# Residual of a Strassen down projection: added in SBUF pages, or by accumulating transfers in DRAM

## The chip, the cores and the metric

The kernel runs on one core of one Trainium2 chip. The metric is the device time of one launch in microseconds (us). A profile of one execution gives the time of every instruction. Engines are named as the profile names them: PE (matrix products; PEld loads its weights), DVE (vector), ACT (scalar), POOL (GpSimd), SP (which only issues transfers here).

## The reference

A decoder block on x of 1024 tokens by 1024 features, all in float32; the part that matters is the SwiGLU layer, which stands at the start and at the end of the block (a mixer of convolution and attention lies between):

```
def swiglu(x, w_gu, w_down):
    g, u = jnp.split(x @ w_gu, 2, axis=-1)
    return (jax.nn.silu(g) * u) @ w_down

u = modulate(rmsnorm(h, norm1_g[l]), mod[:, 0, 0], mod[:, 0, 1])
h = h + FFN_RES_WEIGHT * mod[:, 0, 2][:, None, :] * swiglu(u, ffn1_w_gu[l], ffn1_w_down[l])
...
h = h + FFN_RES_WEIGHT * mod[:, 2, 2][:, None, :] * swiglu(u, ffn2_w_gu[l], ffn2_w_down[l])
return rmsnorm(h, final_g)
```

The hidden width is 2816, 22 tiles of 128. h is the residual.

## The kernel before

Activations lie transposed, features on the 128 partitions and tokens along the free axis. A float32 number is split into a high and a low part for the PE (ACT casts the high part, DVE subtracts it for the low part: `put_split`, L110 to L112), and a product is three matmuls of 512 columns per tile of 128: high by high, high by low, low by high. A high part alone is enough for the first of the three.

SBUF is kept in pages of 128 x 1024 floats, in rings by tag: R has 8 pages, U 16, H 8, X 4. A tile that asks for a page gets the next one of its ring, once its last user is done with it.

Hidden tiles 2 to 21 are worked in ten pairs by Strassen's scheme in Winograd's form: `strassen` makes seven products instead of eight. The seven operands of the moving side are named B11, T2, B21, T3, T1, T4 and B22, in the order of the products. Each product goes to a PSUM bank of one of four tags ("za" has three banks, "fb" two, "dn" two, "st" one), and `u1` (a copy by ACT, L319) to `u4` gather the sums by which the four blocks of the result come out. `sink` takes a block.

`Ffn.pair` makes the hidden tiles of a pair p; `keep(p)` forms their sums in pages called ha, hb, ta and tb (in ring R) and stores the seven operands to DRAM in `hd`. `Ffn.down` is the down projection of these pairs, in three groups: pairs 0 to 3, 4 to 6 and 7 to 9. For a group it loads the seven operands of each pair (L445), splits them, and then runs `strassen` for q = 0 to 3, two tiles of output features each. Names begin with f in the first FFN and s in the second: fB11_0 is operand B11 of pair 0, fd00a to fd00g are the seven split weight blocks for group 0 and q = 0, fd00T1 is the bank of that product, and fd01, fd02, ... follow. POOL makes the sums of weights for each of them (L280, L297, four operations, the first named s3).

The residual lies in the eight R pages while `down` runs: each is loaded in the first group (L457), and `sink` makes a block in three steps: DVE adds two sums (L464), ACT scales by the gate (L465), DVE adds the block to the R page (L466). After the groups the remaining two hidden tiles are done by halves of the tokens (the products named dn): DVE adds each to R (L504), ACT squares, and POOL sums the squares for the norm behind.

The order of the instructions on each engine is set when the program is built, by a scheduler with a timeline of its own that may put a product ahead of another of the same `strassen`; each engine then runs its list in order, and so does SP with the transfers it issues.

## Time and profile before

| what | us |
|---|---|
| median of 3 runs (lowest, highest) | 2101.79 (2100.91, 2103.1) |
| span of the profiled execution | 2098.4 |
| what lies around the span, by the median | 3.4 |
| busy PE, DVE, ACT, POOL in the span | 2039.0, 1600.0, 907.4, 698.1 |
| down projection, groups of the first FFN: from about | 466 to 671 |
| down projection, groups of the second FFN: from about | 1851 to 2053 |

The page gives the profiled execution's span, from its first to its last instruction; its time as a launch is not given apart, so the median stands for it. Busy PE is a modelled figure: matmuls are pipelined. The two stretches of the last lines are where the change works.

### The profile page before, as it was taken

The numbers are of one execution on the slowest core, as the hardware profiler recorded it, in microseconds if no ns is written. First come the engines' busy times: TensorE is split into PE (matmuls) and PEld (weight loads), VectorE is DVE, ScalarE is ACT, GpSimd is POOL, SyncE is SP. The second block draws the span as 40 slices with busy tenths as digits, with TensorE's granted clock in tenths as the row PEclk, the third lists the DMA queues.
The fourth block names the chain that finished last, engine by engine and source line by source line (L and its number), as shares of the span: only waits on it lengthen the run. The fifth ranks groups of instructions, "written<-read, shape, count | busy, mean of one in ns | idle before, by whom it ended". The sixth has DMA issues, their size and how long they took to land.

```text
span 2098.4 us, 26171 instructions
## 1 busy us (share of the span) xinstructions
PE 2039.0 (97%) x8964; PEld 1644.0 (78%) x8964; DVE 1600.0 (76%) x2299; ACT 907.4 (43%) x1601; POOL 698.1 (33%) x510
## 2 busy tenths in 40 slices
PE   7999999999999999999999999999999999999996
PEld 4788888887788788887777788888888888878785
DVE  7858878878998896668876664639766767698998
ACT  4532332353654653226555552337332332355554
POOL 3125455453232333532221100032344444332433
PEclk8999999999999999999999999999999999999998
DMA  8117646565543334244443268321222223375332
GB/s 310 72 56 259 237 181 221 223 218 187 178 143 105 129 146 155 81 119 119 112 138 100 89 233 304 130 108 46 86 95 102 104 101 116 105 278 191 109 97 83
DMA packets 129943, 307.98 MB, mean 147 GB/s; under 512 B 12689, under 2 KB 23057, under 8 KB 129810
## 3 DMA queue, kind: packets, MB, share of 16 engines
q1 hardware_dynamic: 129810, 306.31, 42.2%
q8 instruction: 71, 1.16, 0.2%
q14 instruction: 62, 0.51, 0.1%
HBM read 224.47 MB, written 81.79 MB: 146 GB/s over the span
## 4 chain that ended last, share of the span: by engine, by line
PE 80%; DVE 10%; ACT 3%; issue 3%; DMA 2%; POOL 1%; SPq 0%; DVEq 0%; ACTq 0%; POOLq 0%
PE bga L142 4%; PE bgb L142 4%; PE bo L142 3%; PE z L142 3%; PE byb L142 2%; PE t L851 2%; PE bya L142 2%; PE fbu L142 1%; PE fbg L142 1%; PE o L861 1%; PE o L862 1%; PE sdn L142 1%; DVE wa L204 1%; DVE fT L112 1%; DVE fo L597 1%
## 5 line engine op out<-in xcount | busy, mean ns | idle before, releaser
L830 POOL TENSOR_SCALAR_AFFINE_SELECT a<-a 128x128 f32<-128x128 f32 x64 | 48.2, 761 | 224.7 <-ACT a L730 220.8
L204 DVE SCALAR_TENSOR_TENSOR wa<-wa,cb 128x1024 f32<-128x1024 f32 x72 | 95.6, 1334 | 6.7 <-DMA wa<-in_w_ada_dram 6.7
L833 DVE TENSOR_TENSOR_SCAN r<-r 128x128 f32<-128x128 f32 (+3 forms) x64 | 87.9, 1378 | 1.2
L233 POOL TENSOR_TENSOR acc<-acc,sqc 128x512 f32<-128x512 f32 x14 | 21.0, 1501 | 187.1 <-ACT sqc L232 187.1
L730 ACT ACTIVATE r<-z 128x512 f32<-128x512 f32 (+2 forms) x96 | 47.0, 495 | 53.0 <-PE z L142 52.5
L280 POOL TENSOR_TENSOR fw<-fw 128x512 f32<-128x512 f32 x18 | 29.3, 1626 | 98.0 <-DVE fp10d L112 48.4
L855 ACT CAST ah<-t 128x512 fp32r<-128x512 f32 (+1 forms) x96 | 45.7, 485 | 32.2 <-PE t L851 21.1
L856 DVE TENSOR_TENSOR al<-t,ah 128x512 fp32r<-128x512 f32 (+1 forms) x96 | 51.2, 547 | 9.9 <-ACT ah L855 9.2
L836 DVE TENSOR_TENSOR a<-a,r 128x127 f32<-128x127 f32 (+3 forms) x64 | 48.4, 758 | 10.6 <-POOL a L830 8.6
L465 ACT ACTIVATE fd<-fd,mod 128x512 f32<-128x512 f32 x48 | 34.6, 724 | 35.0 <-DVE fd L464 34.7
L465 ACT ACTIVATE sd<-sd,mod 128x512 f32<-128x512 f32 x48 | 34.6, 723 | 34.9 <-DVE sd L464 34.4
L730 ACT ACTIVATE a<-z 128x512 f32<-128x512 f32 (+2 forms) x96 | 46.7, 497 | 6.5 <-PE t L851 6.3
L280 POOL TENSOR_TENSOR sw<-sw,sw 128x512 f32<-128x512 f32 x20 | 29.1, 1456 | 60.3 <-issue 38.2
L829 DVE TENSOR_TENSOR r<-r,mask 128x128 f32<-128x128 f32 x64 | 18.8, 298 | 39.4 <-ACT r L730 39.2
L851 PE MATMUL t<-ident,a 128*128 128x128 f32 x288 | 48.2, 276 | 0.1
L424 POOL TENSOR_TENSOR sha<-sha,sg 128x512 f32<-128x512 f32 x20 | 34.7, 1734 | 33.4 <-DVE sha L423 33.4
L424 POOL TENSOR_TENSOR shb<-shb,sg 128x512 f32<-128x512 f32 x20 | 30.6, 1532 | 42.3 <-DVE shb L423 42.3
L142 PE MATMUL z<-KB,Q 64*128 64x512 f32 (+2 forms) x96 | 41.2, 435 | 0.5 <-DMA KB<-qk_d 0.5
L947 DVE SCALAR_TENSOR_TENSOR res<-bo,mod,res 128x512 f32<-128x512 f32 x16 | 12.0, 748 | 38.0 <-PE bo L142 38.0
L417 ACT ACTIVATE fg<-fg 128x512 f32<-128x512 f32 x36 | 22.8, 632 | 41.3 <-DVE fg L416 41.1
L851 PEld LDWEIGHTS t<-ident,a 128*128 128x128 f32 x288 | 33.8, 140 | 8.6 <-issue 2.9
L466 DVE TENSOR_TENSOR sr<-sr,sd 128x512 f32<-128x512 f32 x48 | 36.2, 760 | 5.1 <-ACT sd L465 5.0
(3251 smaller groups left out, 6680.3 us busy)
## 6 DMA issues: line engine op xcount, KB each, us to landing
wa<-in_w_ada_dram SPq DMA_DIRECT2D x72, 512.0 KB, 8.3
sw<-in_w_gu_dram SPq DMA_DIRECT2D x40, 512.0 KB, 3.4
fw<-in_w_gu_dram SPq DMA_DIRECT2D x36, 512.0 KB, 4.2
fT<-fhd_d SPq DMA_DIRECT2D x40, 256.0 KB, 5.3
sT<-shd_d SPq DMA_DIRECT2D x40, 256.0 KB, 5.4
qk_d<-qk SPq DMA_DIRECT2D x16, 512.0 KB, 4.5
fB<-fhd_d SPq DMA_DIRECT2D x30, 256.0 KB, 5.9
sB<-shd_d SPq DMA_DIRECT2D x30, 256.0 KB, 5.6
```

The lines of the kernel that those rows point to most:

```text
L142: mm = nc.tensor.matmul(out, l, r, start=first and i == 0, stop=last and i == n - 1)
L204: nc.vector.scalar_tensor_tensor(out=w, in0=w, scalar=1.0, in1=cb, op0=ALU.mult, op1=ALU.mult, accum_out=mods[m][:, nb:nb + 1])
L280: eng.tensor_tensor(out=out, in0=a, in1=b, op=ALU.subtract)
L424: nc.gpsimd.tensor_tensor(out=h[i], in0=h[i], in1=g[i], op=ALU.mult)
L465: act(out=t, in_=t, func=AF.Identity, scale=g)
L730: act_last["silu"] = act(func=AF.Sigmoid, **kw).ins
L830: nc.gpsimd.affine_select(out=a[:, d], in_=a[:, d], pattern=[[-1, P]], compare_op=ALU.is_gt, fill=0.0, base=0, channel_multiplier=1)
L833: nc.vector.tensor_tensor_scan(out=c, data0=c, data1=c, initial=1.0, op0=ALU.mult, op1=ALU.bypass)
L836: nc.vector.tensor_tensor(out=c, in0=c, in1=r[:, tot + 1:tot + W], op=ALU.mult)
L851: act_last['att'] = nc.tensor.transpose(tb[:, (i - 4 * hf) * P:(i - 4 * hf + 1) * P], a[:, off + j * P:off + (j + 1) * P], ident).ins
L855: nc.scalar.copy(out=ah[:, :w], in_=tb[:, c])
L856: nc.vector.tensor_sub(out=al[:, :w], in0=tb[:, c], in1=ah[:, :w].bitcast(F32))
```

## The change

The residual is no longer held in pages during the groups. It stands in DRAM in `res_d` (for the first FFN a copy of x, made by eight transfers from DRAM to DRAM at the start of the pairs; for the second FFN the buffer that the mixer wrote). `sink` loses its third step: POOL issues a transfer that adds the block to its place in DRAM, 48 of them for each FFN, 256 KB each. After the last group the eight R pages are loaded from DRAM, and the tail goes on as before. Operand B11 takes its pages from ring R instead of U.

```
@@ -431,9 +431,10 @@
-        def down(self, src, done, keep=None, final=False):
+        def down(self, res, done, keep=False, final=False):
             n = self.nm
-            tags = dict(self.tags, T1="H", T3="H")
+            tags = dict(self.tags, T1="H", T3="H", B11="R")
@@ -451,11 +452,6 @@
-                    if gi == 0:
-                        for dt in (2 * q, 2 * q + 1):
-                            R[dt] = page("R", f"{n}r{dt}")
-                            dma(out=R[dt], in_=src[dt])
@@ -463,11 +459,14 @@
                         act(out=t, in_=t, func=AF.Identity, scale=g)
-                        nc.vector.tensor_tensor(out=R[dt][:, c], in0=R[dt][:, c], in1=t, op=ALU.add)
+                        nc.gpsimd.dma_start(out=res[dt, :, c], in_=t, accum_op=ALU.add)
                     strassen(*w, k, B, ("za", "st")[q % 2], f"{n}d{gi}{q}", sink)
                 off += 2 * k * P
+            for dt in range(KT):
+                R[dt] = page("R", f"{n}r{dt}")
+                dma(out=R[dt], in_=res[dt])
@@ -503,8 +502,8 @@
-                    if keep is not None:
-                        dma(out=keep[dt, :, c], in_=R[dt][:, c])
+                    if keep:
+                        dma(out=res[dt, :, c], in_=R[dt][:, c])
@@ -618,26 +617,29 @@
+        res_d = dram.tile([KT, P, T], F32, name="res_d")
         for p in range(1, len(PAIRS)):
             f1.pair(p)
             if p < 8:
                 ada(p + 1, "R")
+            else:
+                for kt in range(4 * (p - 8), 4 * (p - 7)):
+                    dma(out=res_d[kt], in_=xT[kt])
-        res_d = dram.tile([KT, P, T], F32, name="res_d")
-        f1.down(xT, norm2, res_d)
+        f1.down(res_d, norm2, keep=True)
```

The last call, `f2.down(res2_d, final, final=True)`, stays as it is.

Outside the down projections no engine's list changes but for the copies at the start and a few products that trade places. Inside, the lists change as follows. On PE, at the first group of the first FFN, before (one row of each product; x3 is high by high, high by low and low by high for one pair):

```order
L142 MATMUL fd00B11_3855<-fB11_0_3705,fd00a_3825 128x512 x3
...
L142 MATMUL fd00T2_3869<-fT2_0_3721,fd00b_3833 128x512 x3
...
L142 MATMUL fd00B21_3883<-fB21_0_3737,fd00d_3836 128x512 x3
...
L142 MATMUL fd00T3_3900<-fT3_0_3753,fd00c_3828 128x512 x3
...
L142 MATMUL fd00T1_3914<-fT1_0_3769,fd00e_3842 128x512 x3
...
L142 MATMUL fd00T4_3932<-fT4_0_3785,fd00f_3845 128x512 x3
...
L142 MATMUL fd00B22_3949<-fB22_0_3801,fd00g_3848 128x512 x3
...
L142 MATMUL fd01B11_4004<-fB11_0_3705,fd01a_3974 128x512 x3
```

and now:

```order
L142 MATMUL fd00T2_3873<-fT2_0_3729,fd00b_3837 128x512 x3
...
L142 MATMUL fd00B21_3887<-fB21_0_3745,fd00d_3840 128x512 x3
...
L142 MATMUL fd00T1_3918<-fT1_0_3777,fd00e_3846 128x512
L142 MATMUL fd00T4_3936<-fT4_0_3793,fd00f_3849 128x512
L142 MATMUL fd00T1_3918<-fT1_0_3777,fd00e_3846 128x512 x2
...
L142 MATMUL fd00T4_3936<-fT4_0_3793,fd00f_3849 128x512 x2
...
L142 MATMUL fd00B11_3859<-fB11_0_3713,fd00a_3829 128x512
L142 MATMUL fd00T3_3904<-fT3_0_3761,fd00c_3832 128x512 x3
...
L142 MATMUL fd00B22_3953<-fB22_0_3809,fd00g_3852 128x512 x3
...
L142 MATMUL fd00B11_3859<-fB11_0_3713,fd00a_3829 128x512 x2
...
L142 MATMUL fd00B11_3859<-fB11_3_3725,fd00a_3829 128x512 x3
L142 MATMUL fd01B11_4004<-fB11_0_3713,fd01a_3974 128x512 x3
```

B11, which was the first of the seven products, is now the last to be finished; T1 and T4 come third and fourth, and d01 begins behind B11.

On SP, from the weights of q = 1 on, before (fr0 to fr4 are residual pages; fta9 and ftb9 the stores of the last pair's sums):

```order
L452 DMA fwd0_3_3968<-in_w_ds1_dram 128x1024
L406 DMA fhd_d_157<-fhb9_3415 128x2x512
L452 DMA fwd0_4_4115<-in_w_ds1_dram 128x1024
L457 DMA fr0_3821<-in_xT_dram 128x1024
...
L457 DMA fr4_4119<-in_xT_dram 128x1024
L406 DMA fhd_d_157<-fta9_3694 128x2x512
L406 DMA fhd_d_157<-ftb9_3695 128x2x512
```

and now:

```order
L453 DMA fwd0_3_3972<-in_w_ds1_dram 128x1024
L406 DMA fhd_d_157<-fhb9_3420 128x2x512
L453 DMA fwd0_4_4115<-in_w_ds1_dram 128x1024
L446 DMA fB11_0_3713<-fhd_d_157 128x512
...
L446 DMA fB11_4_4405<-fhd_d_157 128x512
L406 DMA fhd_d_157<-fta9_3699 128x2x512
L406 DMA fhd_d_157<-ftb9_3700 128x2x512
L446 DMA fB11_5_4409<-fhd_d_157 128x512
L446 DMA fB11_6_4413<-fhd_d_157 128x512
```

The loads of B11 stand where the residual's pages were loaded, and not, as before, as the first of the group; fB11_5 and fB11_6 (group 1) stand behind the stores of ta9 and tb9, since fB11_6 takes the page of ta9.

On ACT, at the same place, now:

```order
L111 CAST fT4_3_3805<-fT4_3_3805 128x512
L111 CAST fT2_4_4417<-fT2_4_4417 128x512
...
L111 CAST fB21_4_4429<-fB21_4_4429 128x512
L111 CAST fB11_0_3713<-fB11_0_3713 128x512
L111 CAST fd01b_3982<-fwd0_2_3970 128x512
...
L111 CAST fB11_3_3725<-fB11_3_3725 128x512
L111 CAST fB11_4_4405<-fB11_4_4405 128x512
...
L111 CAST fd01f_3994<-fwd0_3_3972 128x512
L111 CAST fB11_5_4409<-fB11_5_4409 128x512
L111 CAST fB11_6_4413<-fB11_6_4413 128x512
L319 COPY fd00ot_3855<-fd00B11_3859 128x512
```

Before, the copy fd00ot (u1 of the first product) stood ahead of all this, since its product came first. Now it stands behind the casts of B11 for group 0 and of fB11_4 to fB11_6. On DVE, the low parts follow the same order: behind the last split of T4 stand, up to that of fB11_3, 15 instructions (four splits of group 1, the four sums of `keep(9)`, three weight blocks of d01, four splits of B11); before, 7 stood between there and the last split of the group, fB22_3.

On POOL, where the second group begins, now (fd0311 to fd0312 are the blocks of the last q of group 0):

```order
L462 DMA res_d_901<-fd0311_4335 128x512
L462 DMA res_d_901<-fd0322_4366 128x512
L462 DMA res_d_901<-fd0321_4384 128x512
L462 DMA res_d_901<-fd0312_4401 128x512
L280 TENSOR_TENSOR fd11s3_4621<-fwd1_2_4613,fwd1_3_4615 128x384
L297 TENSOR_TENSOR fwd1_3_4615<-fwd1_3_4615 128x384
L280 TENSOR_TENSOR fwd1_2_4613<-fwd1_3_4615,fwd1_2_4613 128x384
L462 DMA res_d_901<-fd1011_4555 128x512
L280 TENSOR_TENSOR fwd1_2_4613<-fwd1_2_4613 128x384
```

Before, the four transfers and that of fd1011 were not there; the sums of weights for d11 followed those for d10 directly. The second FFN has the same lists with s for f.

## Rows read from the trace of the kernel before

**Rows 1.** The page, parts 1 and 4: busy time by engine, and the chain.

```profile
PE 2039.0 (97%) x8964; PEld 1644.0 (78%) x8964; DVE 1600.0 (76%) x2299; ACT 907.4 (43%) x1601; POOL 698.1 (33%) x510
...
PE 80%; DVE 10%; ACT 3%; issue 3%; DMA 2%; POOL 1%; SPq 0%; DVEq 0%; ACTq 0%; POOLq 0%
```

**Rows 2.** Windows: length, busy PE, PEld, DVE, ACT, POOL, clock, DMA, GB/s.

```profile
475.00:495.00 20.00, 16.63 (x57) 12.06 (x57) 20.00 (x27) 5.08 (x10) 8.22 (x5) 0.83 0.60 218
...
560.00:580.00 20.00, 16.90 (x72) 12.85 (x71) 20.00 (x32) 8.09 (x16) 12.04 (x7) 1.00 0.23 61
...
620.00:640.00 20.00, 18.75 (x81) 14.59 (x81) 20.00 (x32) 7.95 (x15) 9.23 (x6) 1.00 0.29 79
...
1858.00:1878.00 20.00, 16.40 (x67) 11.97 (x66) 20.00 (x26) 5.49 (x10) 8.24 (x6) 1.00 0.61 221
...
1938.00:1958.00 20.00, 16.89 (x66) 12.63 (x65) 20.00 (x33) 9.86 (x20) 9.01 (x4) 0.92 0.26 74
```

**Rows 3.** Timeline of PE, first FFN, first group: start, duration, operation, [idle].

```profile
466.44 2.88 PE L142 MATMUL fd00B<-fB,fd00a 128*128 128x512 f32 x12
...
477.41 0.73 PE L142 MATMUL fd00T<-fT,fd00c 128*128 128x512 f32 x2 [0.38 <-DVE fT L112]
...
483.17 0.73 PE L142 MATMUL fd00T<-fT,fd00e 128*128 128x512 f32 x2 [2.38 <-DVE fT L112]
...
484.85 5.06 PE L142 MATMUL fd00T<-fT,fd00f 128*128 128x512 f32 x11 [0.57 <-DVE fT L112]
...
492.87 2.88 PE L142 MATMUL fd01B<-fB,fd01a 128*128 128x512 f32 x12
```

**Rows 4.** Timeline of DVE in the same stretch.

```profile
481.37 4.64 DVE L112 TENSOR_TENSOR fT<-fT 128x512 fp32r<-128x512 f32 x4
...
486.53 0.68 DVE L112 TENSOR_TENSOR fT<-fT 128x512 fp32r<-128x512 f32 x1
...
490.63 1.28 DVE L112 TENSOR_TENSOR fB<-fB 128x512 fp32r<-128x512 f32 x2
```

**Rows 5.** Timeline of SP, which issues the transfers, in the same stretch.

```profile
481.47 0.33 SPq L452 DMA_DIRECT2D fwd<-in_w_ds_dram  x1
```

**Rows 6.** Timelines of DVE and PE, second FFN, first group.

```profile
1869.47 0.68 DVE L112 TENSOR_TENSOR sT<-sT 128x512 fp32r<-128x512 f32 x1
...
1875.57 2.88 PE L142 MATMUL sd01B<-sB,sd01a 128*128 128x512 f32 x12
```

**Rows 7.** DMA issues of the whole span: count, KB each, median us to landing.

```profile
fB<-fhd_d SPq DMA_DIRECT2D x30, 256.0 KB, 5.9
...
swd<-in_w_ds_dram SPq DMA_DIRECT2D x16, 384.0 KB, 3.1
...
shd_d<-sta SPq DMA_DIRECT2D x10, 512.0 KB, 2.8
...
res_d<-fr SPq DMA_DIRECT2D x16, 256.0 KB, 2.0
...
sr<-res_d SPq DMA_DIRECT2D x8, 512.0 KB, 5.5
```

**Rows 8.** Timelines, second group: POOL and PE (first FFN), PE (second).

```profile
560.71 3.98 POOL L280 TENSOR_TENSOR fd11s<-fwd,fwd 128x384 f32<-128x384 f32 x1 [13.62 <-DMA fwd<-in_w_ds_dram]
...
568.11 0.73 PE L142 MATMUL fd11T<-fT,fd11b 128*128 128x512 f32 x2 [1.40 <-ACT fd11b L111]
...
571.20 0.70 PE L142 MATMUL fd11T<-fT,fd11c 128*128 128x512 f32 x2 [1.70 <-DVE fd10ah L322]
...
1954.50 2.77 PE L142 MATMUL sd11T<-sT,sd11b 128*128 128x512 f32 x7
```

**Rows 9.** Timelines of the tails: POOL (first FFN), ACT and DVE (second).

```profile
679.13 17.89 POOL L233 TENSOR_TENSOR facc<-facc,sqf 128x512 f32<-128x512 f32 x13 [0.68 <-ACT sqf L232]
...
2056.84 0.72 ACT L465 ACTIVATE sd<-sd,mod 128x512 f32<-128x512 f32 x1 [1.42 <-DVE sd L464]
...
2062.72 0.75 DVE L504 SCALAR_TENSOR_TENSOR sr<-sdn,mod,sr 128x512 f32<-128x512 f32 x1 [0.61 <-PE sdn L142]
```


## The prediction

> **What bounds the kernel now.** I read the page first. PE is busy for 2039.0 of the span's 2098.4 us, and the chain that ended last lies on PE for 80% and on DVE for 10% [rows 1]. So a microsecond taken from DVE, ACT or POOL is worth nothing where PE runs without a gap. The places to look for are those where PE waits in the down projections, and windows of 20 us find them: in each the busy time of DVE is to be compared with that of PE [rows 2]. Where a group begins, DVE is full (20.00 of 20) and PE is not: it lacks 3.4 us in the first group of the first FFN and 3.6 in that of the second, 3.1 at each second group, 1.25 at the third group of the first FFN. At the first group of the first FFN and the second group of the second FFN the granted clock falls too (0.83, 0.92). Then the timelines show who is late. In the first group PE waits for the low parts of T3, T1 and T4, one split of DVE each [rows 3], and DVE makes these back to back, 0.60 us apart [rows 4]. Inside a group PE has no such gaps.
>
> **Adds and transfers.** 48 adds of DVE per FFN go. They lie beside PE's products and give nothing by themselves, except at a group's start, counted below. 48 accumulating transfers per FFN come, on POOL. The eight copies of x are issued on SP long before, with PE on the pairs; I cost them at nothing, since no load that is due soon stands behind them on SP's list and their 4 MB have the whole of the pairs to move in; PE's work there is the cover, and a wait of SP in their place would stop the next weights by about what one such transfer takes, some 5.5 for a page [rows 7], which the range's upper end holds.
>
> **The first group.** Here the lists say more than the diff. B11's pages come from ring R, where `keep(9)` still holds pages, so its loads stand behind the weights of q = 1, whose fifth page SP issued at 481.5 us [rows 5]; T2's splits are now the first. What does d00 wait for?
>
> DVE. T4_3's split has as many instructions ahead of it as before (B22's stand there in place of B11's), so it ends at 487.2 again. Behind it stand 15 up to B11_3's: 487.2 + 15 x 0.60 = 496.2, where the last split of the group ended at 491.9 before [rows 4]. PE's last matmuls then end d00 at 496.8; before, d01 began at 492.87 [rows 3]. That alone is +3.9.
>
> PE. Without B11 it runs out of work after T2 and B21, at about 472, until T1's first low part, nine splits ahead of T4_3's end, 481.6. Then 57 matmuls remain: 12.9 us at 0.227 each (12 products take 2.72 from start to start), so 494.5; with eleven of them at the slow pace that followed the shorter waits before (5.06 us for eleven, 0.46 each) 497.1 [rows 3].
>
> ACT. d01's first bank of "za" is the one that the copy fd00ot empties (B11, T3 and B22 of d00 fill all three), and that copy stands behind the cast of fB11_6, whose load waits for the page of fta9. fta9's last sum is the seventh instruction behind T4_3's split: 491.4. Its store takes 2.8, as that of the same tile in the second FFN [rows 7]: 494.2. The load is issued 0.3 later and lands after between 3.1 us (weights) and 5.9 (these operands, where many are queued at once) [rows 7]; with few transfers beside it I take 3.5, the lower end more nearly: 498.0. Two operations of ACT at 0.7 each [rows 9] give 499.4.
>
> The last of the three decides: 499.4 - 492.9 = **+6.5**. In the second FFN T4_3's split ends at 1870.1 and sd01 began at 1875.57 [rows 6]. By the same steps fta is done by 1874.5, the store at 1877.3; ftb's sum, eleventh behind T4_3, and its store's issue stand ahead of the load on SP, so the load goes at 1877.5, lands at 1881, and sd01 begins at 1882.5: **+6.9**. Bounds: DVE alone gives +3.9 and +4.1, with one copy behind it +4.7 and +4.9; a load of 5.9 gives 2.4 more in each, a slow clock on the first eleven matmuls of d01 another 2.6 in each. Together +13.4, between 8 and 23.
>
> **The second and third groups.** While DVE and ACT wait less for loads in group 0, group 1's B11 and four more operands are split there, and the adds are gone. At d11 PE waited 1.40 for fd11b (ACT's, behind POOL's sum fd11s) and 1.70 for DVE's fd10ah [rows 8]. DVE has 40 instructions to do up to there where it had 46: six at 0.60 are 3.6, so the 1.70 goes. The 1.40 I let go by 0.6 only, since four transfers of POOL now stand ahead of fd11s. So 2.3 of 3.1 at the second group of the first FFN, 0.7 of 1.25 at the third, and 2.3 of 3.1 at the second group of the second FFN, where the slow clock goes with the wait: seven matmuls took 2.77 [rows 8], 1.2 more than at 0.227, of which I take 1.0. Sum **-6.3**. At most all of it goes, 3.1 + 1.25 + 3.1 + 1.2 (-8.7), at least the two waits of 1.70 (-3.4).
>
> **The tails.** The residual's last pages are loaded behind the last transfers. The trace has none issued by POOL. From below, a store of the same 256 KB from SP lands in 2.0; from above, it may be a store and a read one after the other, 2.0 + 5.5 = 7.5 [rows 7]. I take 4.5, nearer to the store, with an issue of up to 1.3, what a sum of POOL takes (13 in 17.89) [rows 9], within it. A load of a page alone I take at 4, between 2.0 and 5.5 [rows 7]. In the first FFN PE ends the groups at about 671 and the last block is ready some 2 us behind, at 673, so the page stands at 673 + 4.5 + 4 = 681.6; POOL's chain of sums adds tile 6 at 679.13 + 4 x 1.38 = 684.6 [rows 9] and is what ends last there: nothing. In the second FFN the last scale ended at 2057.6 [rows 9]; without DVE's adds between, it comes 1.5 earlier: 2056 + 4.5 + 4 = 2064.5, and DVE wanted tile 6 at 2062.7 [rows 9]. 1.8 late, of which its waits for PE of 0.6 each take up some: **+1**, between 0 and 6.
>
> **The sum.** +13.4 - 6.3 + 1 = +8.1. The profiled span is 2098.4 and the median of the three runs 2101.79; the 3.4 around the span are not touched, so 2101.8 + 8.1 = 2109.9, and I say 2110.
>
> The Trainium skill (DMA: Bandwidth & Descriptors, "Anatomy of one DMA — SWDGE (gpsimd) path") gives about 2.0 us plus the bytes at 436 GB/s for a transfer issued by GpSimd, an estimate of 2.6 us for 256 KB. No run here shows one. By it the tail of the second FFN would cost nothing and the sum would be 2109.
>
> **Rivals.** A: POOL becomes the bound. In the groups of three pairs a q has seven products of nine matmuls, 63 x 0.227 = 14.3 us, and POOL's work there is 9 to 12 of 20 us [rows 2], 7 to 8 of 14.3; four transfers come on top. If one holds POOL for more than about 1.7 us, POOL falls behind PE. The rows near it run from SP's 0.33 for an issue [rows 5] to 3.98 for a sum of POOL beside a full DVE, where others take 1.3 to 1.4 [rows 8, 9]. At 3 us each a q takes 7.5 + 12 = 19.5 instead of 14.3; over eight such q in each FFN that is 16 x 5.2 = 83 at most, and with some slack left in each group 2130 to 2180. Against it: two blocks of a q can be under way while POOL goes on, if the issue is short as on SP. 0.11.
>
> The Trainium skill speaks for A (SBUF — State Buffer, "SBUF: two separate sides"): GpSimd writes the descriptors of its transfers through a port that DVE can lock, and starves while DVE does. That POOL's sums stretch beside DVE the trace shows (3.98 against 1.3) [rows 8, 9]; whether a transfer's issue does, no run here shows.
>
> B, on the other side: faster. The place is DVE's row of splits ahead of T4_3. There 27 instructions took 20.00 us, 0.74 each [rows 2], where 0.60 is what an undisturbed one needs [rows 4]; the rest falls together with sums of POOL. If the new order keeps them apart, T4_3 is done up to 27 x 0.14 = 3.8 earlier in each FFN, and if fB11_6 lands by DVE's floor as well, the sum is 8.0 - 7.6 - 8.7 + 1 = -7.3, 2094.5; it decides from about 2 us on in each. Against it: POOL makes the same sums of weights in that stretch. 0.14.
>
> C: no change. DVE's floor with one copy behind it decides (+9.6) and the gains come between 6.3 and 8.7: 2101.8 + 9.6 - 8.7 = 2102.7 to 2105.1. It needs fB11_6 by 496 instead of 498.0, a landing in 1.5 us, or a page that comes free earlier. That the change doesn't do what it says at the second groups, since the waits there come back by POOL's weights, is in the forecast's upper part. 0.18.
>
> **How the numbers follow.** The forecast as worked out (2106 to 2124) has 0.57; A 0.11, B 0.14, C 0.18. A measurement of this kernel tells about 0.2% (4.2 us) from no change. Slower is the forecast and A, 0.68; same is C, 0.18; faster is B, 0.14. The range leaves out nearly all of A and half of B: 2096 to 2128. The forecast alone has 2106 to 2124.
>
> **What would show it.** PE's timeline at the first groups: a wait of several us behind B21, and d01's start at 499.4 and 1882.5; then ACT's cast of fB11_6 ahead of fd00ot. At the second groups no wait for fd10ah and some 0.8 for fd11b. POOL's rows: how long an accumulating transfer holds it, and how long it takes to land. In the second FFN's tail a wait of DVE for a load at tile 6. The prediction is wrong if d01 begins before 497, if POOL is late for PE inside a group, or if the tail waits for more than one load.

## The result, and the profile after

The changed kernel takes 2139.77 us, median of four runs (2137.66 to 2141.68), where the kernel before takes 2101.76 beside it: a ratio of 1.0172, 95% interval 1.0156 to 1.0188. The forecast was 2110 with a range of 2096 to 2128; the sign was right, the size was not. The profiled span went from 2098.4 to 2136.7, 38.3 us more. The page after, parts 1, 3, 4 and 5 (to be laid beside [rows 1]):

```profile
PE 2052.4 (96%) x8964; PEld 1649.2 (77%) x8964; DVE 1541.2 (72%) x2203; ACT 910.1 (43%) x1601; POOL 773.4 (36%) x606
...
q0 software_dynamic: 13824, 25.17, 7.7%
...
PE 75%; DVE 11%; DMA 5%; issue 4%; ACT 2%; POOL 2%; SPq 0%; DVEq 0%; POOLq 0%; ACTq 0%
...
L462 POOL DMA_DIRECT2D res_d<-fd x48 | 42.2, 892 | 59.8 <-ACT fd L461 53.6
```

DVE did 59 us less work, as the change means it to. POOL is busy for 36% only, and an accumulating transfer holds it for 0.89 us. What is new in the chain that ended last is DMA, 5% for 2%. Line q0 is the queue of POOL's transfers: their number of packets, megabytes, and the time that they took, as a share of all sixteen DMA engines over the span.

To see where the 38 us lie, I took the start of the first product of each stage from PE's timelines. Each column is the time from one of these starts to the next: group 0, 1 and 2 of each FFN, its tail (first product of dn to the product for the norm, in the second FFN to the end), and between the FFNs the mixer with the second FFN's pairs:

| kernel | start | f g0 | f g1 | f g2 | f tail | between | s g0 | s g1 | s g2 | s tail | span |
|---|---|---|---|---|---|---|---|---|---|---|---|
| before | 466.4 | 83.6 | 61.2 | 59.2 | 19.1 | 1162.1 | 81.2 | 62.9 | 57.4 | 45.4 | 2098.4 |
| change | 467.0 | 92.7 | 57.8 | 63.2 | 28.6 | 1164.9 | 91.3 | 57.8 | 61.6 | 51.9 | 2136.7 |
| difference | +0.6 | +9.1 | -3.4 | +4.0 | +9.5 | +2.9 | +10.0 | -5.1 | +4.2 | +6.5 | +38.3 |

So the second groups gained, by 8.5; the first groups lost 19, the tails 16, the third groups 8. The experiments ran on other chips, six by the numbers on record (7, 14, 11, 0, 8 and 13), where the kernel before takes 2107 to 2109. So each is compared by its ratio to the kernel before on the same chip, and an absolute time that an expectation gives is to be read against 2101.8. The time of a stage comes from one execution, and a part of it is PE's clock: the second group of the first FFN takes 61.2 us in this profile of the kernel before at a granted clock of 1.00, and 63.9 in the one of experiment 12 at 0.95, with PE idle for 3.1 in both. Differences of a stage below 3 us are not read one by one.

**First group.** PE's timeline, then ACT's and SP's (compare [rows 3] and [rows 5]):

```profile
467.04 2.88 PE L142 MATMUL fd00T<-fT,fd00b 128*128 128x512 f32 x12
...
475.15 0.47 PE L142 MATMUL fd00T<-fT,fd00f 128*128 128x512 f32 x1 [2.28 <-DVE fhb L423]
477.94 3.74 PE L142 MATMUL fd00T<-fT,fd00e 128*128 128x512 f32 x9 [2.32 <-DVE fT L112]
...
496.11 2.13 PE L142 MATMUL fd00B<-fB,fd00a 128*128 128x512 f32 x8 [0.78 <-DVE fB L112]
500.85 4.61 PE L142 MATMUL fd01B<-fB,fd01a 128*128 128x512 f32 x12 [2.61 <-ACT fd00ot L319]
```

```profile
499.08 1.24 ACT L111 CAST fB<-fB 128x512 fp32r<-128x512 f32 x2 [3.71 <-DVE fd01f L112]
500.22 0.58 ACT L319 COPY fd00ot<-fd00B 128x512 f32<-128x512 f32 x1
```

```profile
492.48 0.37 SPq L406 DMA_DIRECT2D fhd_d<-fta  x1
494.88 0.37 SPq L406 DMA_DIRECT2D fhd_d<-ftb  x1
495.31 2.99 SPq L446 DMA_DIRECT2D fB<-fhd_d  x3
```

The chain is the one foreseen: store of fta, store of ftb, load of B11 of group 1, its casts, and behind them the copy for which d01 waits 2.61 us. It starts d01 at 500.85 (forecast 499.4), and then d01's first twelve products take 4.61 us in place of 2.88. The granted clock of these 4.61 us is 0.63, so PE was in part at the lower of its two levels, behind waits of 0.78 and 2.61 us; before, it was 1.00 in the same stretch.

**Third group and tails.** The issues and their landing (compare [rows 7]), and pieces of the chain that ended last:

```profile
res_d<-fd POOLq DMA_DIRECT2D x48, 256.0 KB, 5.5
res_d<-sd POOLq DMA_DIRECT2D x48, 256.0 KB, 5.4
...
fwd<-in_w_ds_dram SPq DMA_DIRECT2D x16, 384.0 KB, 5.1
swd<-in_w_ds_dram SPq DMA_DIRECT2D x16, 384.0 KB, 5.0
```

```profile
642.67 4.16 DMA fwd<-in_w_ds_dram
...
657.20 6.22 DMA fwd<-in_w_ds_dram
...
687.27 9.33 DMA res_d<-fd
696.68 3.78 DMA fr<-res_d
700.55 0.76 DVE fr L503
```

The weights of a group, which landed in 3.2 and 3.1 us before, take 5.1 and 5.0, and stand in the chain themselves. PE waits for splits of the third group's operands:

```profile
628.04 0.73 PE L142 MATMUL fd20T<-fT,fd20c 128*128 128x512 f32 x2 [1.32 <-DVE fT L112]
629.71 1.65 PE L142 MATMUL fd20T<-fT,fd20e 128*128 128x512 f32 x6 [0.71 <-DVE fT L112]
```

In the tail the last transfer, issued at 687.27, is landed 9.3 us later; only then is the last of the residual loaded, and PE stands still. That it is issued so late comes from loads and transfers too. ACT has to cast the tail's second tile of weights (fdc1) ahead of the last four scales, and waits for its load; and DVE's last sum waits for a buffer that a transfer still reads:

```profile
680.46 1.05 ACT L98 CAST fdc1h<-fdc1r 128x1024 fp32r<-128x1024 f32 x1 [3.13 <-DMA fdc1r<-in_w_dc_dram]
...
685.48 0.69 DVE L460 TENSOR_TENSOR fd<-fd23ot,fd23B 128x512 f32<-128x512 f32 x1 [0.93 <-DMA res_d<-fd]
```

### The profile page after: what moved, and what is told of

Its sections match the earlier page's. It is cut to its first block, busy times and chain, and to the rows that moved or that the text cites. A ratio compares the mean times of both kernels' runs of the same rounds, so it can differ in the third digit from the quotient of the medians.

```text
span 2136.7 us, 26387 instructions
## 1 busy us (share of the span) xinstructions
PE 2052.4 (96%) x8964; PEld 1649.2 (77%) x8964; DVE 1541.2 (72%) x2203; ACT 910.1 (43%) x1601; POOL 773.4 (36%) x606
## 4 chain that ended last, share of the span: by engine, by line
PE 75%; DVE 11%; DMA 5%; issue 4%; ACT 2%; POOL 2%; SPq 0%; DVEq 0%; POOLq 0%; ACTq 0%
PE bgb L142 4%; PE bga L142 4%; PE bo L142 3%; PE z L142 3%; PE byb L142 2%; PE t L853 2%; PE bya L142 1%; PE fbu L142 1%; PE fbg L142 1%; PE o L863 1%; PE o L864 1%; DMA fwd<-in_w_ds_dram 1%; DVE wa L204 1%; DVE sT L112 1%; DVE fT L112 1%
## 5 line engine op out<-in xcount | busy, mean ns | idle before, releaser
L832 POOL TENSOR_SCALAR_AFFINE_SELECT a<-a 128x128 f32<-128x128 f32 x64 | 48.3, 763 | 226.5 <-ACT a L732 222.6
L280 POOL TENSOR_TENSOR fw<-fw 128x512 f32<-128x512 f32 x18 | 29.3, 1627 | 98.0 <-DVE fp10d L112 48.3
L462 POOL DMA_DIRECT2D res_d<-fd x48 | 42.2, 892 | 59.8 <-ACT fd L461 53.6
L462 POOL DMA_DIRECT2D res_d<-sd x48 | 42.0, 890 | 56.7 <-ACT sd L461 50.2
```

What stands on the lines that cost most here:

```text
L280: eng.tensor_tensor(out=out, in0=a, in1=b, op=ALU.subtract)
L462: nc.gpsimd.dma_start(out=res[dt, :, c], in_=t, accum_op=ALU.add)
L832: nc.gpsimd.affine_select(out=a[:, d], in_=a[:, d], pattern=[[-1, P]], compare_op=ALU.is_gt, fill=0.0, base=0, channel_multiplier=1)
```

## The experiments

The question after the result: is it B11's place, the wait for what the transfers write, the room that they take from other loads, or POOL? The stages of most of them stand in one table at the end.

**1. The residual's loads freed from the transfers.** Edit (src is x, then the mixer's output; the blocks still go to res_d, and the first FFN's result to a tensor of its own):

```
-                dma(out=R[dt], in_=res[dt])
+                dma(out=R[dt], in_=src[dt])
```

> Edit: the eight residual pages are loaded from a tensor that no transfer adds to (x in the first FFN, the mixer's output in the second), so their loads wait for pages alone; the transfers go on as in the change, into res_d. Left out: what the pairs add to the residual. Theory (the tails wait for the last transfers to land, then load): the first FFN's tail loses its 9.5 us and the second's its 6.6, less what is left of the loads themselves: 2124 to 2127 instead of 2139.8. Rival (the tails are slow because the transfers keep the DMA engines full, whatever is waited for): less than 5 us come back, 2135 or more.

Measured: ratio 1.0151 (1.0134 to 1.0168). The tails are back at 19.1 and 46.2, so their loss hangs on this wait. Yet nothing clear came back in the whole, 0.06% against the change on these chips (1.0157 in experiment 13): SP now issues the eight pages as early as pages come free, inside the groups, where they land in 8.9 us, and the weights land later than in the change (6.0):

```profile
fwd<-in_w_ds_dram SPq DMA_DIRECT2D x16, 384.0 KB, 6.0
...
fr<-in_xT_dram SPq DMA_DIRECT2D x8, 512.0 KB, 8.9
```

The groups lost what the tails gave back (f g1 62.7, f g2 65.6). Read against 2101.8 the ratio gives 2133.5, between the theory and the rival; the tails did what the theory says, the whole did not.

**2. Plain stores.** Edit: `accum_op=ALU.add` goes, nothing else.

> Edit: the same 96 transfers from POOL at the same places, but as plain stores that do not add; every engine's list is word for word that of the change. Left out: the residual's old value and the sum (the block overwrites its place). Theory (an adding transfer costs more of the DMA engines than a store of the same bytes: 1.7 us of all sixteen, and 5.5 us to landing): each lands in 2.5 to 3.5, the tails give back 2 to 3 us each, the loads for the third group are on time and give back up to 4 each: 2126 to 2134. Rival (what costs is that POOL issues and SP's list is as it is, not the adding): within 3 us of 2139.8.

Measured: 1.0046 (1.0031 to 1.0061), less than the theory allowed. The same lists, issues and bytes without the adding, and most of the loss is gone: third groups 58.1 and 57.1, tails 19.9 and 48.3.

```profile
q0 software_dynamic: 7680, 25.17, 3.1%
...
L462 POOL DMA_DIRECT2D res_d<-fd x48 | 26.4, 551 | 66.7 <-ACT fd L461 57.3
```

```profile
res_d<-fd POOLq DMA_DIRECT2D x48, 256.0 KB, 3.4
...
fwd<-in_w_ds_dram SPq DMA_DIRECT2D x16, 384.0 KB, 3.6
```

Per transfer: 80 packets instead of 144, 0.68 us of all sixteen engines (3.1% of 2116.6 over 96) instead of 1.71 (7.7% of 2136.7 over 96), 3.4 us to landing instead of 5.5.

**3. B11 back in U.** Edit: `T3="H", B11="R"` becomes `T3="H"`.

> Edit: B11 takes its pages from ring U as before the change; the accumulating transfers stay, ring R stands empty during the groups. Nothing is left out. Theory (the first group loses 9.7 and 10.0 us because B11's pages in ring R come free late): these go, and of the gains at the second group (3.4 and 5.1) a half stays, since DVE's adds are gone: 2120 to 2128. Rival (the first group is slow because of the transfers' traffic or POOL's issues): 2135 to 2140.

Measured: 1.0163 (1.0148 to 1.0178), a miss: the rival's time, though not for its reason. The first groups are as before (87.7 and 81.0, with 87.7 and 81.2 in experiment 12), so their loss is indeed B11's; but the second groups take 64.3 and 64.2 and the third 65.3 and 65.7, and all is spent again. What B11 in R costs in the first group it gives back in the others.

**4. No transfers.** Edit: the line with the transfer goes.

> Edit: sink ends after the scale, no block is transferred anywhere; the residual pages are loaded after the groups from res_d as in the change. Left out: what the pairs add. Theory (tails and third groups lose by the transfers, the first groups by B11): 2139.8 - 16 - 8 = 2116, with the first groups' 20 us still lost. Rival (the third group loses by the order of SP's list, the weights of d21 ahead of its operands): 2124, the 8 us there still lost.

Measured: 1.0025 (1.0016 to 1.0035), 2113 where the expectation, put on this chip, says 2122. First groups 96.8 and 89.1, all second and third ones 57.1 to 57.2, PE's own pace (4 x 63 x 0.227): the third group's loss is the transfers', not SP's order.

**5. The transfers alone.** Edit, on the kernel before, beside DVE's add (x is copied to scr_d as in the change):

```
                        nc.vector.tensor_tensor(out=R[dt][:, c], in0=R[dt][:, c], in1=t, op=ALU.add)
+                       nc.gpsimd.dma_start(out=scr_d[dt, :, c], in_=t, accum_op=ALU.add)
```

> Edit: the kernel before with its residual in pages and B11 in U, and beside DVE's add the same 96 adding transfers from POOL into a scratch tensor that nobody reads (x is copied there as in the change). Nothing is left out. Theory (the adding transfers' traffic alone makes the loads of weights and operands late): ratio to before 1.006 to 1.011, with the loads of the weights at 5 to 6 us instead of 3.1 and the loss at the second and third groups. Rival (only waits for what the transfers write cost, loads of the residual in the tails above all): ratio under 1.002.

Measured: 1.0186 (1.0169 to 1.0203), more than expected and more than the change itself, though nothing but a later transfer to the same place depends on what these write. An engine can wait for them only where it writes again to the buffer that they read, and DVE waited so once, for 0.3 us. POOL's sums of weights now stand behind transfers that wait for ACT's scale; kernel 2 has that order too, and there it costs, with the plain stores, 0.21% over kernel 4. The weights land in 4.5 and 4.4, not in the 5 to 6 that were expected. Second groups 69.2 and 69.8, third 65.3 and 65.4; the tails lose 3.1 and 5.2 too. PE waits where the second group begins:

```profile
566.47 2.84 PE L142 MATMUL fd10T<-fT,fd10c 128*128 128x512 f32 x8 [3.50 <-DVE fT L112]
```

The wait begins at a load. ACT sat idle for the load of an operand of that group, and DVE for ACT; the third line is DVE at the same place in the kernel before (experiment 12), and from there on its splits run one behind the other in both:

```profile
550.06 0.62 ACT L111 CAST fB<-fB 128x512 fp32r<-128x512 f32 x1 [4.89 <-DMA fB<-fhd_d]
550.71 0.69 DVE L112 TENSOR_TENSOR fB<-fB 128x512 fp32r<-128x512 f32 x1 [4.82 <-ACT fB L111]
...
547.28 1.37 DVE L112 TENSOR_TENSOR fB<-fB 128x512 fp32r<-128x512 f32 x1 [1.62 <-ACT fB L111]
```

The trace also tells whether POOL's issues slow DVE. In the groups of the first FFN, DVE's two-input operations of 128x512 took 0.68 us on average where an issue of POOL ran beside them (61 of them), and 0.68 where POOL was idle (103); only beside POOL's sums of weights they took 0.99.

**6, 7. DVE adds in the third group.** Edit, on the change; the tag of B11 is U, R, U by group in the first kernel, R, R, U in the second:

```
+                    if gi == 2:
+                        for dt in (2 * q, 2 * q + 1):
+                            R[dt] = page("R", f"{n}r{dt}")
+                            dma(out=R[dt], in_=res[dt])
...
+                        if gi < 2:
                             nc.gpsimd.dma_start(out=res[dt, :, c], in_=t, accum_op=ALU.add)
+                        else:
+                            nc.vector.tensor_tensor(out=R[dt][:, c], in0=R[dt][:, c], in1=t, op=ALU.add)
```

> Edit: adding transfers for the first two groups alone; in the third the residual's pages are loaded and DVE adds as before the change; B11 in ring U for the first and third group, in R for the second. Nothing is left out. Theory: the tails' 16 us go, the first groups' loss by B11 goes, a part of the gain at the second group stays, some delay by the traffic stays: ratio 1.000 to 1.005. Rival (the traffic in the first two groups is enough to make the third late): 1.008 or more.

> Edit: as the kernel with adding transfers for two groups and DVE's adds in the third, but with B11 in ring R for the first group too, as in the change. Nothing is left out. Theory: 0.3 to 0.5% above that kernel, by the first groups' late B11, so ratio 1.004 to 1.009. Rival (what is lost at the first group comes back at the second, as B11 in U for all groups showed no gain): the same as that kernel within 0.2%.

Measured: 1.0154 (1.0137 to 1.0171) and 1.0144 (1.0129 to 1.0159); both times the rival came out. The tails are at 19.0 and 45.5, and the third groups at 69 in all four. SP's list goes with it: the first residual loads wait there for transfers to land, and T3 and T1 stand behind them. SP's waits, and PE's, in the first of the two:

```profile
SPq L459 <- DMA res_d<-fd: 31.6, 4, 9.1
```

```profile
637.85 1.95 PE L142 MATMUL fd20T<-fT,fd20c 128*128 128x512 f32 x3 [4.97 <-ACT fT L111]
```

The wait was moved from the tail to the third group. As the second's rival said, the first group's B11 changes nothing in the sum.

**8. No transfers, first group's B11 in U.** Edit: as in 4, with the tags U, R, R for B11 by group.

> Edit: no transfer of blocks at all, and B11 in ring U for the first group, in R for the others. Left out: what the pairs add. Theory (the first groups' 13 and 8 us without transfers are B11's late pages): they go for the most part, ratio 0.994 to 0.998 against 1.0025 with B11 in R throughout. Rival (what the first group gives back is lost again at the second, whose operands are then not split ahead): 1.001 to 1.003.

Measured: 0.9945 (0.993 to 0.996), as the theory said: 87.3, 57.1, 57.4 and 80.8, 57.7, 58.9. The room that the residual leaves and the adds that DVE is spared are together worth 0.55%, if it cost nothing to bring the residual elsewhere; the two were not told apart.

**9. Three tiles only.** Edit, on the kernel before; the pages of `ahead` are B11's in group 1, and ring R gives them to tiles 5 to 7 afterwards:

```
+            ahead = [page("R", f"{n}B11_{p}", F32R) for p in GROUPS_DN[1]]
...
+                        if gi == 0 and dt < 5:
                             R[dt] = page("R", f"{n}r{dt}")
                             dma(out=R[dt], in_=src[dt])
+                        if gi == 2 and dt >= 5:
+                            R[dt] = page("R", f"{n}r{dt}")
+                            dma(out=R[dt], in_=res[dt])
...
+                        if dt < 5 or gi == 2:
                             nc.vector.tensor_tensor(out=R[dt][:, c], in0=R[dt][:, c], in1=t, op=ALU.add)
+                        else:
+                            nc.gpsimd.dma_start(out=res[dt, :, c], in_=t, accum_op=ALU.add)
```

> Edit: from the kernel before. Ring R holds five residual pages (tiles 0 to 4, added by DVE as before the change) and, in its other three, B11 of the second group, loaded and split during the first; the blocks of tiles 5 to 7 go by adding transfers in the first two groups (12 per FFN instead of 48), and in the third these tiles' residual is loaded into the three pages and DVE adds. B11 of the first and third group in U. Nothing is left out. Theory (room for operands ahead is worth 4 to 6 us at each second group, and the cost grows with the number of adding transfers, some 0.3 to 0.4 us each): -10 + 5 to 9 us, ratio 0.995 to 1.000. Rival (a few adding transfers at the groups' ends already make the loads late): 1.003 or more.

Measured: 1.0035 (1.0022 to 1.0049), the rival. Second groups 63.1 and 62.2, so no gain from B11 ahead; third 62.5 and 61.7, with SP held for 11.6 us by the transfers in front of the residual's loads.

**10. Weights in R.** Edit, on kernel 3: `page("WR", ...)` becomes `page("R", ...)` for the weights.

> Edit: the change, with B11 in ring U and the weights of the down projections in ring R (eight pages instead of WR's three). Nothing is left out. Theory (inside the groups the adding transfers cost because the next weights, and what stands behind them on SP's list, land late with only three pages to load ahead into): most of the loss at the second and third groups goes, the tails stay: ratio 1.007 to 1.011 against 1.0163 with B11 in U and weights in WR. Rival (the operands' loads are late by the traffic itself): 1.014 or more.

Measured: 1.0117 (1.0103 to 1.0131), between the two. Second groups 57.5 and 58.7, and both tails as short as before, which the theory did not expect; but the first weights wait for R's pages, and PE with them:

```profile
485.79 1.22 PE L142 MATMUL fd00B<-fB,fd00a 128*128 128x512 f32 x2 [17.30 <-ACT fd00a L111]
```

**11. Two plain stores for each block.** Edit:

```
-                        nc.gpsimd.dma_start(out=res[dt, :, c], in_=t, accum_op=ALU.add)
+                        nc.gpsimd.dma_start(out=res[dt, :, c], in_=t)
+                        nc.gpsimd.dma_start(out=scr_d[dt, :, c], in_=t)
```

> Edit: the change with two plain stores from POOL in place of each adding transfer, one to the residual's place and one to a scratch tensor: about as much time of the DMA engines (2 x 0.68 us against 1.71), twice the issues on POOL. Left out: the residual's old value and the sum. Theory (what slows the loads is the share of the DMA engines that the transfers take): near the change, ratio 1.011 to 1.018. Rival (it is the adding itself, through its landing time and what waits for it): near that with one plain store, 1.0046 to 1.008.

Measured: 1.0105 (1.0089 to 1.012), just under the theory's range and well above the rival's. They take 6.1% of the engines' time, 1.35 us per block. Stores that nobody waits for but the buffers slow the second groups to 62.3; with one store these were at 57.7. The rest up to the change lies in the tails (21.6 and 47.1, where the adding has 27.8 and 53.2).

**12, 13. The kernels before and after, unchanged, on the chips of the experiments.**

> The kernel before, unchanged, for its profile on this chip, which the other profiles of these runs are to be laid beside. All theories: the first group of the first FFN starts d01 within 1 us of 492.9 and the span is within 0.4% of 2098.4.

> The change, unchanged, on the chip of the experiments. All theories: ratio 1.0155 to 1.0190. If the chip's own state sets the first group of the first FFN, it takes 96 to 98 us here from d00 to d10, as with plain stores, against 92.7 in the first profile; the other stages within 1.5 us of that profile: second groups 57 to 59, third 62 to 65, first tail 27 to 30.

Measured: 2109.33 and span 2107.6 for the first, a miss in both parts: it does not start d01 at 492.9 but at 501.8, and its span is 0.44% longer. Of the 9 us, 5 lie ahead of d00 and are of this execution, since kernels 9 and 11 start d00 at 468.1 on the same chip; 4 lie in the first group, which takes 87 to 89 us in every kernel here that has B11's first group in U (10 and 15 apart, whose first weights lie in R). The change has a ratio of 1.0157 (1.0136 to 1.0177) here; the second groups and the first tail are within the bounds named, the first group (95.6) and the third ones (61.7 and 60.8) up to 1.2 under them.

**14 to 16. Only the later weights in R.** Edits on kernel 10: `page("R" if gi else "WR", ...)`; `page("R" if gi or q else "WR", ...)`; and the first of these with plain stores.

> Edit: the change, with B11 in ring U; the weights of the first group in their own three pages, those of the second and third in the eight pages of ring R. Nothing is left out. Theory (late weights are what the adding transfers cost inside the groups): no wait at the starts, the second groups at 57 to 59 us, the third at 59 to 62, the tails as short as before: ratio 0.996 to 1.002. Rival (the operands are late by the traffic, and the gain of the second group only moves): 1.006 or more.

> Edit: as the kernel with the first group's weights in their own pages, but only those of its first q; from q = 1 on the weights go to ring R. Nothing is left out. Theory: R's pages come free when the last pair's sums are stored, so d01 of each FFN waits for weights that its own ring would have loaded earlier: 5 to 12 us above that kernel. Rival (the weights of q = 1 come in time from R too, and later ones earlier): the same within 0.2%.

> Edit: as the kernel with the first group's weights in their own pages and the others in R, with plain stores in place of the adding transfers; every engine's list is the same. Left out: the residual's old value and the sum. Theory (with the weights early the adding costs little inside the groups): 0.1 to 0.4% below that kernel, from the third groups. Rival (the adding still costs as in the change): 1% or more below it.

Measured: 1.007 (1.0058 to 1.0083), 1.0036 (1.0023 to 1.005) and 0.9989 (0.998 to 0.9998). In the first, third groups (60.9 and 61.5) and tails (19.1 and 45.8) are better than in kernel 3 by 4.4, 4.2, 8.9 and 7.1: this much of the loss hangs on weights and what SP has behind them. In the first FFN's tail the residual's loads wait for the last transfer as in the change, but it is issued 2.0 us behind dn's first product (685.06), and the load follows 6.3 later:

```profile
687.05 0.86 POOL L462 DMA_DIRECT2D res_d<-fd  x1 [1.18 <-ACT fd L461]
...
693.37 0.81 SPq L468 DMA_DIRECT2D fr<-res_d  x2
```

But the second groups stand at 65.7 and 66.2, no better, and PE waits there for operands:

```profile
570.76 3.78 PE L142 MATMUL fd10T<-fT,fd10c 128*128 128x512 f32 x8 [3.93 <-DVE fT L112]
```

The ratio is the rival's. With plain stores and the same lists they take 62.0 and 61.4, the third 57.4 and 57.1; the ratio is 0.8% lower, where the theory said 0.1 to 0.4% and the rival 1% or more, so with the weights ahead too the adding costs most of what it costs in the change (0.8 against 1.1, which lie between kernel 2 and the change). The second kernel was expected to be slower and is faster: its d01 waits for weights (first groups 95.2 and 86.9), and in the 40 us ahead of the second group DVE makes 10 of its operands' splits, where the first kernel has 3 (second groups 58.6 and 57.8).

**17, 18. Tiles 0 to 2 by transfers instead of 5 to 7.** Edits on kernel 9: `dt < 5` becomes `dt >= 3` and `dt >= 5` becomes `dt < 3`; then, in the second, transfers in the third group too, and the three loads behind it.

> Edit: as the kernel with three tiles by adding transfers (12 per FFN, B11 of the second group in three pages of R), but for tiles 0 to 2 in place of 5 to 7, so that the transfers fall into the first half of a group and not onto the loads of the next group's operands. Nothing is left out. Theory (the adding transfers cost where they meet the operands' loads): the second groups at 57 to 59 us instead of 63.1 and 62.2, the third at 58 to 61 with the residual's three loads ahead of operands: ratio 0.996 to 0.999. Rival (number and bytes count, not the place): 1.002 to 1.005, as with tiles 5 to 7.

> Edit: as the kernel with tiles 0 to 2 by adding transfers, but in all three groups (18 per FFN), and these three pages are loaded behind the groups, as in the change. Nothing is left out. Theory: the operands of the third group no longer stand behind the residual's loads on SP, third groups at 57 to 59, and the tails stay as before since the last of these transfers is issued two q ahead of the end: ratio 0.994 to 0.998. Rival (a load behind the last transfers makes the tail late again, as with 48): 1.001 or more.

Measured: 1.0023 (1.0013 to 1.0033) and 1.0046 (1.0032 to 1.006). The third groups of the first kernel are as before (57.1 and 58.3), but the second ones are worse (67.3 and 64.4), so the place in the group is not what counts there. In the second kernel the tails are as before (19.0 and 45.3), so its rival's time came out, but not its reason. None of the versions that leave nothing out beats the kernel before. In the first, PE's waits at d11 are those of the kernel before, 1.36 and 1.70; new are small waits for DVE ahead of them:

```profile
571.47 0.74 PE L142 MATMUL fd10T<-fT,fd10e 128*128 128x512 f32 x2 [0.71 <-DVE fT L112]
...
573.74 0.96 PE L142 MATMUL fd10B<-fB,fd10g 128*128 128x512 f32 x3 [0.84 <-DVE fd10g L112]
```

What makes DVE late there was not tested by itself.

| kernel (the chips of the experiments) | f g0 | f g1 | f g2 | f tail | s g0 | s g1 | s g2 | s tail | ratio |
|---|---|---|---|---|---|---|---|---|---|
| before | 87.7 | 63.9 | 57.1 | 19.0 | 81.2 | 61.8 | 59.0 | 45.4 | 1 |
| change | 95.6 | 58.1 | 61.7 | 27.8 | 91.3 | 58.9 | 60.8 | 53.2 | 1.0157 |
| 1 residual not behind transfers | 97.0 | 62.7 | 65.6 | 19.1 | 91.1 | 62.5 | 63.7 | 46.2 | 1.0151 |
| 2 plain stores | 97.2 | 57.7 | 58.1 | 19.9 | 91.5 | 57.7 | 57.1 | 48.3 | 1.0046 |
| 3 B11 in U | 87.7 | 64.3 | 65.3 | 28.0 | 81.0 | 64.2 | 65.7 | 52.9 | 1.0163 |
| 4 no transfers | 96.8 | 57.1 | 57.1 | 19.0 | 89.1 | 57.1 | 57.2 | 44.7 | 1.0025 |
| 5 before, with transfers | 88.5 | 69.2 | 65.3 | 22.1 | 82.4 | 69.8 | 65.4 | 50.6 | 1.0186 |
| 8 none, first B11 in U | 87.3 | 57.1 | 57.4 | 19.0 | 80.8 | 57.7 | 58.9 | 44.7 | 0.9945 |
| 11 two plain stores | 96.1 | 62.3 | 57.1 | 21.6 | 89.8 | 62.4 | 57.1 | 47.1 | 1.0105 |
| 14 later weights in R | 87.2 | 65.7 | 60.9 | 19.1 | 80.8 | 66.2 | 61.5 | 45.8 | 1.007 |

## Why the prediction was wrong

**Adds and transfers: the step that failed.** The prediction took the 48 transfers of each FFN as beside everything, and asked of them only how long they hold POOL and when the last one lands. What they take from the loads it put at nothing, without a reason. They take 1.71 us of all sixteen DMA engines each; with four in every 14.3 us, and the loads of weights and operands on the same engines, the weights land in 5.1 instead of 3.2. The DMA share of the second and third group of the first FFN, the last number but one in each line, doubles. These are, in this order, the kernels before and after the change, no transfers, plain stores, two plain stores, and the transfers alone:

```profile
550.00:670.00 120.00, 115.66 (x504) 93.73 (x503) 110.97 (x182) 66.76 (x126) 39.91 (x28) 1.00 0.38 122
560.00:680.00 120.00, 116.05 (x502) 93.10 (x501) 83.40 (x136) 60.12 (x114) 56.90 (x59) 1.00 0.78 178
565.00:678.00 113.00, 113.00 (x501) 93.55 (x500) 83.85 (x137) 61.46 (x116) 30.82 (x28) 1.00 0.42 140
565.00:680.00 115.00, 114.28 (x502) 93.64 (x501) 84.10 (x138) 61.77 (x117) 47.77 (x60) 1.00 0.56 189
565.00:683.00 118.00, 114.75 (x499) 94.53 (x499) 84.90 (x137) 62.25 (x116) 65.66 (x92) 0.99 0.77 268
556.00:690.00 134.00, 121.61 (x504) 94.46 (x503) 118.76 (x186) 72.84 (x137) 64.37 (x61) 0.97 0.78 185
```

The transfers alone, beside the unchanged kernel, cost 1.86% (kernel 5); without them the change is at 1.0025 (kernel 4), so they are 1.32 of the 1.57% that it lost on those chips. It is the adding, not POOL, nor the order: plain stores with the same lists stand at 1.0046. Waits for the buffers that the transfers read are 0.3 us of DVE in kernel 5 and 0.9 in the change, and DVE is no slower beside an issue. Above kernel 4, one plain store per block (0.68 us of the engines) costs 0.21%, two (1.35) 0.80%, the adding one (1.71) 1.32%: the loss rises with the engines' time, faster than in proportion, and what sets the change apart from two stores lies in the tails. Two stores also write twice the bytes, and an adding one has to read what it adds to; so the engines' time and the memory's were not told apart.

**The tails: right chain, two terms too small.** Forecast 0 and +1, measured +9.5 and +6.5. The chain (last transfer, load, DVE) is as described, and the load itself took 3.8 where 4 was taken. The last transfer took 9.3 us to land, not 4.5, above the bound of 7.5 too: it landed among loads of weights for the next stage and of residual pages. DVE waited for three loads of the residual, 9.0 us in all, where the prediction named more than one as a sign of being wrong. And the transfer was issued 6.6 us behind dn's first product (687.27 - 680.65) instead of 2.7 (673 against 670.3 of before). Kernel 1 shows that the loss of the tails hangs on this wait (19.1 and 46.2 without it). Kernel 14 shows that the wait by itself need not cost: with the weights ahead the last transfer is issued 2.0 behind dn's first product, the load follows 6.3 later, within the forecast's bounds, and the tails lose 0.1 and 0.4. So most of this loss hangs on late loads as well.

**Third groups: not foreseen.** The prediction had -0.7 and 0; measured +4.0 and +4.2. Operands for the third group stand behind weights on SP's list, and those wait for pages that late weights free late. Against kernel 3, kernel 14 gives 4.4 and 4.2 back by weights ahead; that the remainder is the operands' own lateness is likely but not shown.

**First groups: right in mechanism, the size within the bounds.** Forecast d01 at 499.4 and 8 to 23 us lost in the two; measured 500.85, and 9.1 + 10.0 = 19.1. Of the missing 5.7, 3.5 are the slower pace of d01's first products (1.7 and 1.8, held as a bound of 2.6 each); the other 2.2 lie on the way to the copy: counted from the stage's start, fta's store went out 0.5 and 1.1 later than reckoned, and the loads behind it took the rest. ftb's store, which the forecast counted for the second FFN, cost nothing: in both the loads follow fta's store by 2.83 (492.48 to 495.31, and 1898.37 to 1901.20), the 2.8 that this store was given. DVE's floor fell about where it was put: the last splits of B11 let PE go on at 496.1.

**Second groups: right in sign.** -2.3 and -3.3 were forecast, -3.4 and -5.1 measured, somewhat above what was put as the most (3.1, and 3.1 + 1.2). Both waits went whole in the first FFN, that for fd11b too, which was let go by 0.6 only: PE is busy there for 56.9 of the 57.0 us from 560 to 617.

**Between the FFNs** 2.9 us were lost in the first profile and 3.6 in the second; with plain stores it was 0.9, but with kernel 3, which has the adding transfers, 0.9 as well. Nothing was tried for it, and it stays open.

**The rivals.** A, POOL as the bound, is out: a transfer holds POOL for 0.89, half of the 1.7 at which it would decide. What the Trainium skill says of GpSimd and DVE (SBUF — State Buffer, "SBUF: two separate sides"), that DVE in a two-port mode locks GpSimd out while it writes descriptors, does not show here: the longest of the 48 issues of the first FFN took 1.49 us, the median one 0.87. Whether any of DVE's operations there ran in such a mode the traces do not tell. The Trainium skill's 2.0 us plus bytes (DMA: Bandwidth & Descriptors, "Anatomy of one DMA — SWDGE (gpsimd) path") gives 2.6 as an estimate; plain stores from POOL landed in 3.1 to 3.4 among other transfers, adding ones in 5.4 to 5.5. B and C did not occur (C's sum also left out the +1 of the tails). That the change does what it says in the second group is shown by kernel 8: without the transfers, and with the first group's B11 where it was, the second groups take 57.1 and 57.7, and the whole gains 0.55%.

## What to carry to other kernels

A transfer that takes work from an engine is not free because it runs beside it: count its time on the DMA engines (packets, share), and ask which loads then come late and how many pages they can be ahead. A load that must wait for a transfer to land should stand last on its queue, since everything behind it waits too; moving such a wait (kernels 6, 7, 9) moves the loss. And where DVE is the limit at a group's start, time lost in one group can be time saved in the next (kernels 3 and 15): sum the stages before calling one of them a gain.

## What the runs showed of the hardware

An adding transfer of 256 KB from SBUF to DRAM takes 144 packets and 1.71 us of the sixteen engines, a plain one from the same queue 80 and 0.68. It holds POOL for 0.89 us instead of 0.55. It lands in 5.5 us, 9.3 where residual pages and weights are loaded beside it; and 96 of them beside an otherwise unchanged kernel cost 1.86% of its time. DVE's float32 operations on 128x512 took 0.68 us with such an issue beside them as without, and 0.99 beside POOL's sums (kernel 5).
